# A hybrid attention encoder layer on one core: branch A's values as plain products kept on chip, branch B's rows stored in group order and merged by two heads and two tiles

## The chip, the core and the metric

The kernel runs on one core of a Trainium2 chip. The metric is the device time of one execution in microseconds (us). The engines are TensorE (PE in the profile: matrix products and transposes, with PEld its weight loads), VectorE (DVE), ScalarE (ACT), GpSimd (POOL) and SyncE (SP, which here only issues DMAs). Each engine works through its own queue in order and waits on semaphores; DMAs are issued from SP's and POOL's queues and move data between the chip's memory and DRAM.

## What is computed

The reference is one layer of an encoder on 1024 sample rows and 256 prompt rows of width 1024, in fp32:

```python
h = _rmsnorm(x, g_mix)
z = h @ w_in                                   # queries, keys, values of A and B, and 2 x 1024 gates
gates = jax.nn.sigmoid(z[..., o6:] + b_gate)
o_a, _ = _banded_attention(qa, ka, va, 128, 1, rel_bias[:, :8], sink)
o_b = _dilated_mixture(qb, kb, vb, rel_bias[:, 8:])
merged = gates[:, :, 0] * (o_a @ w_branch_a) + gates[:, :, 1] * (o_b @ w_branch_b)
x = x + merged @ w_out
h = _rmsnorm(x, g_mlp)
x = x + jnp.square(jax.nn.relu(h @ w_up)) @ w_down
return _rmsnorm(x, g_final)
```

Branch A has 8 heads of 64 in two groups that share keys and values, a window of 128 to both sides, and a sink. Branch B has three groups of four heads with dilations 1, 4 and 16; the group's sequence is taken apart by residues, each residue sees a band, and the three groups' outputs are mixed per head and row with a softmax of their log sums:

```python
alpha = jax.nn.softmax(jnp.stack(lses), axis=0)
o = jnp.sum(alpha[..., None] * jnp.stack(outs), axis=0)
```

## The kernel before

The 1280 rows are ten tiles of 128 (eight of the sample, two of the prompt) or three blocks of 512, 512 and 256 columns once transposed. fp32 accuracy comes from splitting: a value is rounded to fp32r by ScalarE (`split`, L184), the rest is taken by VectorE (L185), and a product is three fp32r products (low x high, high x low, high x high; `mm3`, L191). A matrix product on fp32 tiles without the split is called plain here.

The stages, by their place in the span: the norm and the value columns of w_in (0 to 120 us; `evac` writes the values to DRAM, A's split into two parts in scr_va, B's in scr_vb); 14 pairs of 128-column blocks of w_in (120 to 472; `PAIRS` at L46, `pair` at L805) which give queries, keys and 11 of the 16 gate blocks, each written to DRAM from a stage tile z; attention (472 to 876); branch B's product with w_branch_b and its gate (876 to 904); the out projection and norm (904 to 1060); the MLP (1060 to 1832). `entering` (L467) runs at the hooks of the last pair: it loads the first unit's queries and keys on SP, the normed input h, and prepares the first plain gate's weights (`prepare`: the load into raw, the ScalarE part L231, the VectorE part L235).

Attention is a list of 100 tiles: ten units of ten tiles, a unit being two heads. Units 0 to 3 are branch A, 4 and 5 are group 0 of branch B, 6 and 7 group 1, 8 and 9 group 2. For each tile `scores` (L890) multiplies queries and keys (L908 and L909 for A, L911 for B), adds the bias with the row maximum on VectorE (L915), negates the maximum (L920, L924) and takes the exponential on ScalarE (L926); one tile later `transposes` (L931) turns the probabilities on TensorE (L942) and evacuates them, and one more tile later `values_of` (L951) multiplies them with the values. A's values are [high | low] of 64 columns each as the stationary side and split probabilities as the moving one, 256 wide, two products per block of 128 keys (L962). The two halves of the output are added by ScalarE and VectorE (L968, L969), and the transposed result is stored by POOL into scr_a (L970). B's are plain products of 64 columns (L977), copied (L264 or L262, taken in turn) into o of 132 columns (two heads and the row's maximum and sum), which POOL stores into scr_b at strided rows (L986) or scr_b0 (L990). s has four buffers, o three.

Between the three steps of each tile a counter, `tick` (L1125), advances other work by hand-written rules. `logits` (L1005) are the products of the five gate blocks left over (11 to 15): 360 matmuls in 45 steps of eight, spread over tiles 0 to 39. From tile 42 on `sums_a` (L992) makes the reciprocal sums l_a and stores them transposed to scr_l; `fetch_gates` (L1040) loads the gates into mT; `fetch_a` (L1019) loads A's outputs and sums back on POOL's queue, multiplies them (L1036) and splits them into ohi and olo; `branch_a` (L1047) multiplies with w_branch_a and the gates (L1059). From tile 94 on `tail` (L1110) merges the three groups for one tile of 128 rows at a time: `merge` (L1063) loads r in two DMAs, takes minima, exponentials and weights on small tiles (L1071 to L1081), three products and two sums of 256 columns (L1085, L1092, L1093); `turn_merged` (L1099) transposes and splits. Most merges run after the last tile. The loop at L1183 multiplies with w_branch_b, columns outside and blocks inside, and applies the gates (L1194, L1196), with gate tiles sg loaded four steps ahead by SP (L1172).

Tiles live in pools with a fixed number of slots (tags m, w and q, of 4, 4 and 1 KB a partition). The order of instructions from the start of attention to the second half of the out projection is made by the scheduler from the program's order; ahead of that and behind it the program's order is kept.

Of the kernel before, what the change touches and what calls it, by code (L numbers as in the profile page):

```python
# [45 lines left out]
PAIRS = [(0, OFF_G), (P, OFF_G + P), (2 * P, OFF_G + 2 * P), (3 * P, OFF_G + 3 * P), (512, OFF_G + 4 * P)]  # L46
PAIRS += [(off + 256 * g, off + 256 * g + P) for g in (2, 1, 0) for off in (OFF_K, OFF_Q)]
PAIRS += [(OFF_G + P * c, OFF_G + P * c + P) for c in (5, 7, 9)]
# [48 lines left out]
def encoder_kernel(  # L97
# [155 lines left out]

    nm_a = const.tile([P, AH, NT], F32, name="nm_a")
# [14 lines left out]
    scr_a = dram.tile([AH * HD, T], F32, name="scr_a")  # L269
    scr_l = dram.tile([AH, T], F32, name="scr_l")  # L270
    scr_b = dram.tile([T, 2, 2, ROW], F32, name="scr_b")
# [118 lines left out]
    scr_va = dram.tile([T, 4 * HD], F32, name="scr_va")  # L390
    scr_vb = dram.tile([T, 3 * BH * HD], F32, name="scr_vb")
# [10 lines left out]
    def load_unit(u):  # L402
        st = {}
        if u < 4:
# [3 lines left out]
            if u % 2 == 0:  # L408
                kk = [slot("kk", (P, NS), F32R) for _ in range(2)]
                for i in range(2):  # L410
                    for r in HALVES:
                        nc.sync.dma_start(kk[i][r, :].bitcast(F32), scr_ka[g, i, :, :NS])
                        nc.sync.dma_start(shared["kp"][r, 2 * g + i, :].bitcast(F32), scr_ka[g, i, :, NS:])
                shared["k"] = [Pair(kk[i], shared["kp"][:, 2 * g + i, :]) for i in range(2)]
            if u:
                st["q"] = [Chunk("q", F32R) for _ in range(2)]
            else:
                rest = slot("qp", (P, 2, NP), F32R)
# [5 lines left out]
            if u == 0:  # L424
                shared["v"] = [slot("va", (P, 4 if t < 8 else 2, 2, 2, HD), F32R) for t in range(0, NT, 4)]
                for i, v in enumerate(shared["v"]):
                    src = scr_va[512 * i : min(T, 512 * i + 512), :].rearrange("(t p) c -> p t c", p=P)
                    nc.sync.dma_start(v.rearrange("p t g a d -> p t (g a d)").bitcast(F32), src)
# [8 lines left out]
        cols = slice(256 * g + P * i, 256 * g + P * i + P)  # L437
        sample, rest = scr_vb[:NS, cols], scr_vb[NS:, cols]
# [28 lines left out]
    def entering():  # L467

        nonlocal unit0
        yield  # L470
# [6 lines left out]
        yield  # L477
# [22 lines left out]
    with ExitStack() as pre:  # L500
# [99 lines left out]
        def evac(t, v, ps):  # L600
            rows = slice(P * t, P * t + P)
            vo = own("vo", (P, 512), n=2)
            if v == 0:
                nc.vector.tensor_copy(vo, ps)
                nc.gpsimd.dma_start(scr_vb[rows, :512], vo)
                return
            va = own("va", (P, 2, 2, HD), F32R, 2)
            split(va[:, :, 0, :], va[:, :, 1, :], ps[:, :P].rearrange("p (g d) -> p g d", g=2))
            nc.gpsimd.dma_start(scr_va[rows, :], va.rearrange("p g a d -> p (g a d)").bitcast(F32))
            nc.scalar.activation(vo[:, : 2 * P], ps[:, P : 3 * P], AF.Copy)  # L610
            nc.gpsimd.dma_start(scr_vb[rows, 512:], vo[:, : 2 * P])
# [100 lines left out]
    with ExitStack() as pre:  # L712
# [5 lines left out]
        class Rows:  # L718
# [5 lines left out]
            def begin(self):  # L724
                self.z = stage("z", (P, T), n=3)
# [19 lines left out]
        class Parts:  # L745
# [5 lines left out]
            def begin(self):  # L751
                self.z = [stage("z", (P, T), F32R, n=3) for _ in range(2)]
# [17 lines left out]
        class Gate:  # L770
# [5 lines left out]
            def begin(self):  # L776
                self.z = stage("z", (P, T), n=3)
# [80 lines left out]
    with ExitStack() as pre:  # L858
# [21 lines left out]
        def rows_out(g, n, gi):  # L880

            step = STEPS[g][gi >= NS]
            base, length = (0, NS) if gi < NS else (NS, NP)
            r, j = divmod(gi - base, length // step)
            first = base + r + step * j
            return slice(first, first + step * (n - 1) + 1, step)

        live, units = {}, {}

        def scores(u, t, tile):  # L890
# [4 lines left out]
            s = a3("s", bufs=4)  # L895
            m = small.tile([P, 2], F32, name="m", tag="m")
            o = a3("o", (P, ROW))
# [33 lines left out]
        def transposes(u, t, tile):  # L931
            W = tile[1]
            s, o = live[u, t]
            pt = a3("pt", (P, 6, P), bufs=2, dt=F32R if u < 4 else F32)
            low = wslot("pl", (P, 6, P), F32R) if u < 4 else None
# [13 lines left out]
            live[u, t] = (pt, low, o)  # L949

        def values_of(u, t, tile):  # L951
            st = units[u][0]
            pieces, W, _ = tile
            pt, low, o = live.pop((u, t))
            nb = W // P
            pv = bank("pv")
            if u < 4:
                for b in range(nb):
                    k = pieces[0][3] // P + b
                    v = st["v"][k // 4][:, k % 4, u // 2].rearrange("p a d -> p (a d)")  # L960
                    for p in (low, pt):
                        nc.tensor.matmul(  # L962
                            pv[:, : 2 * P], v, p[:, 2 * b : 2 * b + 2, :].rearrange("p h q -> p (h q)"),
                            start=b == 0 and p is low, stop=b == nb - 1 and p is pt,
                        )
                for h in range(2):
                    r, q = HALVES[h], slice(P * h, P * h + P)
                    nc.scalar.activation(o[r, :P], pv[HALVES[1], q], AF.Copy)  # L968
                    nc.vector.tensor_tensor(o[r, :P], pv[HALVES[0], q], o[r, :P], op=ALU.add)  # L969
                nc.gpsimd.dma_start(scr_a[P * u : P * u + P, P * t : P * t + P], o[:, :P])  # L970
                return
            g, i = divmod(u - 4, 2)
            for h in range(2):
                vc = HALVES[h]
                for p0, n, qa, ka in pieces:
                    for b in range(nb):
# [5 lines left out]
                        )  # L982
# [687 lines left out]
```

## Time and profile before

| | us |
|---|---|
| median of 3 runs | 1831.42 (1829.44 to 1832.73) |
| the profiled execution | 1833.65 |
| its span, first to last instruction | 1831.9 |
| TensorE busy | 1757.1 (96%), mean granted clock 0.970 |
| VectorE busy | 1000.4 (55%) |
| ScalarE busy | 754.9 (41%) |
| GpSimd busy | 528.1 (29%) |
| DMA | 255.46 MB in 187512 packets |

A share of busy time is a mean over stages that have different limits; the views by window show one stage at a time. Matmuls are pipelined, so the mean duration of one is longer than the time from one to the next, and a busy TensorE is not one at its peak. PEclk is the share of full speed that TensorE's clock was granted.

### The profile page before, as it was taken

The page shows a single profiled execution, that of the slowest core. Times are in us where ns is not written, and L with a number is a line of the kernel's source. Part 1 is how long each engine was busy: PE and PEld are TensorE (multiplying, and loading weights), DVE is VectorE, ACT ScalarE, POOL GpSimd, SP SyncE. Part 2 cuts the span into 40 slices and gives each one's busy share as a digit, 9 for nine tenths or more (in the row PEclk, how much of TensorE's full clock was granted, in tenths as well). Part 3 has the DMA queues.
Part 4 walks back from the last instruction along what each step waited for, and adds up shares of the span by engine and source line. Part 5 has one row for each costly group of instructions (what it writes and reads, how often), then busy time and mean ns, then how long its engine had stood idle before and what let it go on. Part 6 is the DMA issues. An engine that isn't in the chain of part 4 may idle for free.

```text
span 1831.9 us, 24545 instructions
## 1 busy us (share of the span) xinstructions
PE 1757.1 (96%) x9001; PEld 1464.9 (80%) x9001; DVE 1000.4 (55%) x1768; ACT 754.9 (41%) x1594; POOL 528.1 (29%) x438
## 2 busy tenths in 40 slices
PE   7999999999799989997899799999999999999998
PEld 6898888888688866765688688888888888888886
DVE  6633333322377743448846844554554796658575
ACT  6233332223376733543516533333333433233345
POOL 0221332212011231231010145555555551215050
PEclk9999999999899976998899999999999999999999
DMA  6416443332834574115611133444433864633433
GB/s 230 138 48 198 142 125 98 95 104 88 278 96 146 197 212 148 47 37 178 234 54 79 60 113 119 142 147 147 135 123 123 302 240 128 231 125 104 125 123 115
DMA packets 187512, 255.46 MB, mean 139 GB/s; under 512 B 15303, under 2 KB 116379, under 8 KB 187264
## 3 DMA queue, kind: packets, MB, share of 16 engines
q1 hardware_dynamic: 176576, 225.62, 37.7%
q0 software_dynamic: 9728, 26.18, 4.5%
q10 hardware_dynamic: 1088, 2.10, 0.3%
q8 instruction: 71, 1.16, 0.3%
q14 instruction: 49, 0.40, 0.1%
HBM read 167.66 MB, written 91.43 MB: 141 GB/s over the span
## 4 chain that ended last, share of the span: by engine, by line
PE 51%; DVE 4%; ACT 2%; DMA 2%; issue 1%; POOL 0%; SPq 0%; DVEq 0%; POOLq 0%; ACTq 0%
PE dn L345 19%; PE x L345 9%; PE mm L191 7%; PE pv L345 5%; PE z L345 4%; PE y L345 2%; PE sc L911 2%; PE pv L977 2%; PE pt L942 1%; DMA scr_b<-o 1%; DMA raw<-in_w_down_dram 0%; DVE ulo L185 0%; DMA raw<-in_w_out_dram 0%; DVE clo L312 0%; DVE sg L1194 0%
## 5 line engine op out<-in xcount | busy, mean ns | idle before, releaser
L345 PE MATMUL dn<-dhi,ulo 128*128 128x512 f32 x448 | 174.6, 390 | 2.7 <-DVE ulo L185 2.7
L376 POOL TENSOR_TENSOR tb<-raw 128x512 f32<-128x512 f32 x30 | 39.0, 1301 | 473.0 <-DMA raw<-in_w_in_dram 170.1
L312 DVE TENSOR_TENSOR wlo<-ta,whi 128x1024 fp32r<-128x1024 f32 x30 | 56.6, 1887 | 215.7 <-ACT whi L310 215.7
L345 PE MATMUL dn<-dlo,uhi 128*128 128x512 f32 x448 | 174.3, 389 | 0.0
L345 PE MATMUL dn<-dhi,uhi 128*128 128x512 f32 x448 | 174.3, 389 | 0.0
L345 PE MATMUL x<-chi,wlo 128*128 128x512 f32 x424 | 167.3, 395 | 6.9 <-ACT phi L184 6.9
L345 PE MATMUL x<-clo,whi 128*128 128x512 f32 x424 | 167.0, 394 | 0.0
L345 PE MATMUL x<-chi,whi 128*128 128x512 f32 x424 | 166.3, 392 | 0.0
L312 DVE TENSOR_TENSOR wlo<-raw,whi 128x1024 fp32r<-128x1024 f32 x60 | 93.2, 1553 | 111.1 <-ACT whi L310 111.1
L345 PE MATMUL pv<-phi,wlo 128*128 128x256 f32 x480 | 135.6, 283 | 0.9 <-ACT u L1558 0.9
L345 PE MATMUL pv<-phi,whi 128*128 128x256 f32 x480 | 135.8, 283 | 0.0
L345 PE MATMUL pv<-plo,whi 128*128 128x256 f32 x480 | 135.8, 283 | 0.0
L915 DVE CUSTOM_DVE_ANT_0 s<-sc,bias 128x256 f32<-128x256 f32 (+2 forms) x200 | 77.5, 404 | 64.4 <-PE pt L942 29.4
L185 DVE TENSOR_TENSOR ulo<-uraw,uhi 128x1024 fp32r<-128x1024 f32 x56 | 95.1, 1718 | 11.7 <-ACT uhi L184 11.7
L345 PEld LDWEIGHTS dn<-dhi,ulo 128*128 128x128 f32 x448 | 84.1, 188 | 21.3 <-DVE ulo L185 3.8
L345 PEld LDWEIGHTS x<-chi,wlo 128*128 128x128 f32 x424 | 80.7, 190 | 22.9 <-ACT phi L184 7.3
L345 PEld LDWEIGHTS dn<-dlo,uhi 128*128 128x128 f32 x448 | 84.1, 188 | 17.4
L345 PEld LDWEIGHTS dn<-dhi,uhi 128*128 128x128 f32 x448 | 84.1, 188 | 17.3
L345 PEld LDWEIGHTS pv<-phi,wlo 128*128 128x128 f32 x480 | 91.9, 191 | 3.4 <-ACT u L1558 1.1
L345 PEld LDWEIGHTS x<-chi,whi 128*128 128x128 f32 x424 | 80.5, 190 | 17.2
L345 PEld LDWEIGHTS pv<-plo,whi 128*128 128x128 f32 x480 | 91.9, 191 | 2.3
L345 PEld LDWEIGHTS x<-clo,whi 128*128 128x128 f32 x424 | 80.7, 190 | 15.1
(329 smaller groups left out, 4607.0 us busy)
## 6 DMA issues: line engine op xcount, KB each, us to landing
scr_u<-u SPq DMA_DIRECT2D x112, 320.0 KB, 2.6
uraw<-scr_u SPq DMA_DIRECT2D x56, 512.0 KB, 4.6
raw<-in_w_in_dram SPq DMA_DIRECT2D x33, 512.0 KB, 5.1
raw<-in_w_up_dram SPq DMA_DIRECT2D x32, 512.0 KB, 5.2
raw<-in_w_down_dram SPq DMA_DIRECT2D x28, 512.0 KB, 6.2
uraw<-scr_u SPq DMA_DIRECT2D x28, 256.0 KB, 4.4
scr_g<-z SPq DMA_DIRECT2D x11, 640.0 KB, 7.6
scr_qa<-z SPq DMA_DIRECT2D x16, 320.0 KB, 6.5
```

The costliest lines, as they stand in the source:

```text
L185: nc.vector.tensor_tensor(lo, src, hi.bitcast(F32), op=ALU.subtract)
L191: nc.tensor.matmul(ps, a, b, start=i == 0, stop=i == len(seq) - 1)
L312: nc.vector.tensor_tensor(lo, src, hi.bitcast(F32), op=ALU.subtract)
L345: nc.tensor.matmul(ps, a, b, start=first and i == 0, stop=last and i == len(seq) - 1, skip_group_check=True)
L376: nc.gpsimd.tensor_tensor(tb[:, 0], b12, b11, op=ALU.subtract)
L911: nc.tensor.matmul(ps[p0 : p0 + n, :W], st["q"][rows, qa : qa + n], st["k"][rows, ka : ka + W], start=True, stop=True,)
L915: nc.vector.tensor_tensor_reduce(s[:, h, :W], ps[:, :W], bias[:, h, c0 : c0 + W], 1.0, -3.0e38, op0=ALU.add, op1=ALU.max, accum_out=m[:, h ...
L942: nc.tensor.transpose(ps[:, P * (i % 4) : P * (i % 4) + P], s[:, h, P * b : P * b + P], ident)
L977: nc.tensor.matmul(pv[p0 : p0 + n, HD * h : HD * h + HD], pt[:, 2 * b + h, p0 : p0 + n], v_at(st, ka // P + b)[:, vc], start=b == 0, stop= ...
```

## The change

- The order of the pairs in `PAIRS`: queries of A pair with each other, and gates 1 to 10 pair at the end. The stage tile z has four buffers in place of three.
- The values of A and B go to one DRAM tensor (scr_v) with one copy and one store per tile, A's no longer split.
- `entering` issues the load of the first plain gate's weights at the first hook, ahead of the loads of unit 0, and prepares one hook earlier. Six steps of `logits` (48 matmuls) are taken ahead of the first scores. The other 39 are spread over tiles 0 to 59 in place of 45 over tiles 0 to 39.
- A's values are plain products of 64 columns, 208 where there were 208 of 256 columns; the probabilities are copied and not split. The result goes into rows on chip (`oa`, five m slots for two tiles each) and not to scr_a. `turn_a` scales the rows by l_a on VectorE, transposes them (four per tile) and splits them from PSUM into ohi and olo. scr_a, scr_l and `fetch_a` are gone.
- `window` runs `turn_a` and `branch_a` densely from tile 62 on, every step to tile 73 and two of five after that; `branch_a` goes by block and half of the columns.
- The order of units is 0, 1, 2, 3, 8, 6, 4, 9, 7, 5, so that the first heads of the three groups are done after tile 69 and the second heads at the end.
- B's rows are stored in the order in which the group's tiles produce them; `merge(i, t)` merges one pair of heads for two tiles of 128 rows, with r of [rows, two tiles, three groups]: 76 loads of r where there were 20, two products of 384 columns and two sums of 256 in place of three and two of 256, ten merges as before. The turned columns are put back in order by a strided split, 20 of 128 columns in place of ten of 256. The first pair of heads is merged in tiles 74 to 97, the second from tile 95 on.
- o is made only for branch B, s has three buffers. The branch-B loop has blocks outside and columns inside, and both halves of w_branch_b are fetched ahead.

The core of the diff:

```diff
     def entering():
         nonlocal unit0
+        fetch()
         yield
         unit0 = load_unit(0), *load_bias(0, wslot)
...
-        yield
         prepare()
         yield
...
             for i, e, ps in banks:
-                dst, src = pt[:, i:e, :], ps[:, : P * (e - i)].rearrange("p (i q) -> p i q", q=P)
-                if u < 4:
-                    split(dst, low[:, i:e, :], src)
-                else:
-                    copy(dst, src)
+                copy(pt[:, i:e, :], ps[:, : P * (e - i)].rearrange("p (i q) -> p i q", q=P))
...
             for h in range(2):
-                vc = HALVES[h]
+                vc = HALVES[h if u >= 4 else u // 2]
                 for p0, n, qa, ka in pieces:
                     for b in range(nb):
                         nc.tensor.matmul(
...
+            if u < 4:
+                copy(oa(t)[:, P * u : P * u + P], pv[:, :P])
+                return
             copy(o[:, : 2 * HD], pv[:, : 2 * HD])
             for p0, n, qa, ka in pieces:
                 if g:
-                    nc.gpsimd.dma_start(scr_b[rows_out(g, n, qa), g - 1, i, :], o[p0 : p0 + n, :])
+                    nc.gpsimd.dma_start(scr_b[g - 1][qa : qa + n, i, :], o[p0 : p0 + n, :])
...
+        def turn_a(t):
+            if t in (0, 4, 8):
+                o_hi.block(t // 4)
+                o_lo.block(t // 4)
+            o = oa(t)
+            o3 = o.rearrange("p (h d) -> p h d", h=AH)
+            nc.vector.tensor_tensor(o3, o3, l_a[:, :, t].unsqueeze(2).to_broadcast([P, AH, HD]), op=ALU.mult)
+            yield
+            ps = bank("pt")
+            for k in range(4):
+                nc.tensor.transpose(ps[:, P * k : P * k + P], o[:, P * k : P * k + P], ident)
+            p3 = ps.rearrange("p (k q) -> p k q", k=4)
+            per = o_hi.per(P * t)
+            for k in range(0, 4, per):
+                split(o_hi.at(k, P * t, P, per), o_lo.at(k, P * t, P, per), p3[:, k : k + per, :])
+            yield
...
+        def window():
+            for t in range(4):
+                yield from turn_a(t)
+            w_as[0] = weight()
+            w_as[1] = weight(0)
+            for b in range(3):
+                turns = then(*[turn_a(t) for t in range(4 * b + 4, min(4 * b + 8, NT))])
+                for _ in branch_a(b, range(4)):
+                    yield
+                    steps_of(turns, 2)
+                    yield
+            w_as[2] = weight(0)
+            w_as[3] = weight(0)
+            for b in range(3):
+                yield from branch_a(b, range(4, KC))
...
+        def merge(i, t):
+            r = wslot("r", (P, 2, 3, ROW))
+            for j in range(2):
+                if t < 8:
+                    a = P // 8 * (t + j)
+                    src = scr_b0[t + j][:, i, :].rearrange("(q m) c -> m q c", m=8), (
+                        scr_b[0][:NS, i, :].rearrange("(r q m) c -> m r q c", r=4, m=2)[:, :, a : a + 16]), (
+                        scr_b[1][:NS, i, :].rearrange("(r q) c -> r q c", r=8)[:, a : a + 16])
+                    for m in range(2):
+                        nc.sync.dma_start(r[64 * m : 64 * m + 64, j, 1, :], src[1][m])
+                    nc.sync.dma_start(r[:, j, 2, :], src[2])
+                    nc.sync.dma_start(r[:, j, 0, :], src[0])
+                    continue
...
+            for j in range(2):
+                o = r[:, j, :, : 2 * HD].rearrange("p g (h d) -> p g h d", h=2)
+                nc.vector.tensor_tensor(o, o, e[:, j].unsqueeze(3).to_broadcast([P, 3, 2, HD]), op=ALU.mult)
+            m = a3("mg", (P, 2, P), bufs=2)
+            nc.vector.tensor_tensor(m, r[:, :, 0, : 2 * HD], r[:, :, 1, : 2 * HD], op=ALU.add)
+            nc.vector.tensor_tensor(m, m, r[:, :, 2, : 2 * HD], op=ALU.add)
...
-        order = [(u, t, tile) for u in (0, 1, 2, 3, 8, 9, 6, 7, 4, 5) for t, tile in enumerate(tiles_of(u))]
+        order = [(u, t, tile) for u in (0, 1, 2, 3, 8, 6, 4, 9, 7, 5) for t, tile in enumerate(tiles_of(u))]
...
         def tick(i):
             n = ticks[0]
             ticks[0] += 1
-            if i < 40:
-                if (n + 1) * 45 // 120 > n * 45 // 120:
+            if i < 60:
+                if (n + 1) * 39 // 180 > n * 39 // 180:
                     next(fill, None)
-            elif i > 44:
-                if n % 3 == 0 and n < 168 or n % 9 == 0 and ticks[0] < 300:
-                    next(side)
-                if i > 94 or i == 94 and n % 3 == 2:
-                    next(last, None)
+                return
+            if i > 61 and (i < 74 or n % 5 < 2):
+                next(side, None)
+            if 74 <= i < 98:
+                if n % 3 == 1:
+                    next(merges[0], None)
+            if done[0] < 20 and i > (94, 96, 98, 99, 101)[done[0] // 4]:
+                next(merges[1])
+                done[0] += 1
...
+        steps_of(fill, 6)
```

More of the change, by code (lines that the diff above doesn't have):

```diff
@@ L953, in values_of @@
             pieces, W, _ = tile
-            pt, low, o = live.pop((u, t))
+            pt, o = live.pop((u, t))
             nb = W // P
             pv = bank("pv")
[L957 to L971, printed above, removed]
             g, i = divmod(u - 4, 2)
             for h in range(2):
-                vc = HALVES[h]
+                vc = HALVES[h if u >= 4 else u // 2]
                 for p0, n, qa, ka in pieces:
```

220 lines of the change are left out of this document (85 added, 135 removed).

## The prediction

> **What bounds the kernel now.** I read the page's slices first (TensorE is busy nearly everywhere, but its clock dips around attention), then the busy time by stage from the view of windows, then the timeline and the chain of waits at the two places where TensorE stands still.
>
> ```profile
> core 0: us, PE busy (x) PEld busy (x) DVE busy (x) ACT busy (x) POOL busy (x), PEclk, DMA share, GB/s
> 120.00:472.00 352.00, 352.00 (x1856) 300.50 (x1855) 110.91 (x115) 110.47 (x160) 85.60 (x73) 1.00 0.40 124
> 472.00:490.00 18.00, 6.34 (x23) 5.02 (x22) 2.17 (x6) 3.28 (x4) 1.47 (x2) 0.62 0.89 311
> 490.00:640.00 150.00, 147.56 (x933) 127.37 (x931) 107.23 (x366) 109.66 (x321) 24.38 (x44) 1.00 0.47 153
> 640.00:700.00 60.00, 51.98 (x213) 37.18 (x211) 30.93 (x115) 25.71 (x88) 20.62 (x34) 0.75 0.65 192
> 700.00:760.00 60.00, 58.03 (x321) 39.52 (x320) 22.69 (x113) 24.16 (x85) 13.82 (x25) 0.80 0.35 105
> 760.00:847.00 87.00, 86.21 (x558) 62.85 (x558) 44.65 (x218) 42.92 (x144) 28.53 (x54) 1.00 0.26 71
> 847.00:880.00 33.00, 18.08 (x76) 13.26 (x75) 25.41 (x92) 6.33 (x15) 0.05 (x1) 0.66 0.62 210
> 880.00:904.00 24.00, 24.00 (x124) 20.53 (x123) 21.87 (x40) 13.02 (x24) 0.00 (x0) 0.97 0.88 290
> ```
>
> The stages outside 472 to 904 us are full of products that the change leaves alone: in 120 to 472 TensorE is busy for 352.00 of 352.00 us at clock 1.00. The change there only reorders column pairs and stores the values in another form, so I cost it at nothing; the cover is TensorE itself, and without it the values' store, the only part with less work, would gain, not cost. All of the sum comes from the attention stage and its two ends. There TensorE is held up in three places: at the start (6.34 us busy of 18), in the first part of branch B (clock 0.75 and 0.80), and in the merges (18.08 of 33).
>
> **The start of attention.** These rows are from the timeline; columns are start, duration, engine, line, and in brackets the idle time before.
>
> ```profile
> 482.02 1.06 ACT L231 ACTIVATE whi<-raw 128x1024 fp32r<-128x1024 f32 x1 [13.88 <-DMA raw<-in_w_in_dram]
> 484.38 0.79 PE L191 MATMUL mm<-hhi,wlo 128*128 128x512 f32 x1 [11.66 <-DVE wlo L235]
> 487.66 0.42 DVE L915 CUSTOM_DVE_ANT_0 s<-sc,bias 128x256 f32<-128x256 f32 x1 [3.33 <-DMA scr_g<-z]
> ```
>
> The weights of the first plain gate arrive late, ScalarE waits for them with the last pair's sigmoid queued behind, and the store of that gate (scr_g) holds the first eviction until 487.66. The change issues this load at the first hook, ahead of SP's loads of unit 0, so both steps come earlier. 48 of the 360 gate products are put ahead of the first scores; at 24 x 0.227 + 24 x 0.113 (prices below) they take 8.2 us, and they cover the loads of unit 0. From 472.7 I expect about 10 us to the first eviction, so 483: **-5 us**. If unit 0's loads are still the last to land it is 0; if they were early, -7, since the 8.2 us remain in the way.
>
> **Branch A's tiles (490 to 640).** First the prices. The first two rows are windows of TensorE alone, the next ones the timeline of a branch-B tile, then one row of the chain of waits in branch B, the rest groups in 490 to 640.
>
> ```profile
> 1600.00:1800.00 200.00, 199.26 (x880) 1.00 0.36 115
> 150.00:450.00 300.00, 300.00 (x1586) 1.00 0.39 121
> 815.09 0.49 PE L942 MATMUL pt<-ident,s 128*128 128x128 f32 x3
> 815.51 0.45 PE L977 MATMUL pv<-v,pt 128*64 128x64 f32 x8
> 815.89 0.50 PE L191 MATMUL mm<-ohi,wlo 128*128 128x512 f32 x1
> 817.18 1.10 PE L977 MATMUL pv<-v,pt 128*128 128x64 f32 x8
> 818.22 0.49 PE L911 MATMUL sc<-k,q 64*128 64x256 f32 x2
> 729.69 1.90 PE pv L977 x8
> L962 PE MATMUL pv<-pl,va 128*128 128x256 f32 x103 | 28.7, 305 | 1.7 <-DVE o L969 0.9
> L962 PE MATMUL pv<-pt,va 128*128 128x256 f32 x102 | 25.9, 281 | 0.0
> L191 PE MATMUL mm<-hhi,whi 128*128 128x512 f32 x76 | 30.9, 406 | 0.0
> L191 PE MATMUL mm<-plo,whi 128*128 128x256 f32 x40 | 11.8, 294 | 0.0
> L185 DVE TENSOR_TENSOR pl<-pt 128x512 fp32r<-128x512 f32 x40 | 27.6, 689 | 15.4 <-ACT pt L184 14.7
> L969 DVE TENSOR_TENSOR o<-pv,o 64x128 f32<-64x128 f32 x78 | 21.9, 281 | 10.6 <-ACT o L968 9.5
> ```
>
> The mean durations of matmuls overlap, so I price by rate. All matmuls of 1600 to 1800 are 512 wide: 200 / 880 = 0.227 us. In 150 to 450 they are two 512-wide to one 256-wide, 300 / 1586 = 0.189, which leaves 0.113 for a 256-wide one. A plain fp32 product is not one record: lines 973 to 980 issue four for a tile of two blocks, the trace shows x8, and from 817.18 to the next start at 818.22 they take 1.04 us, so 0.26 us for each 128x64 product. That is more than twice the 0.113 of the 256-wide fp32r product that it replaces. The change replaces 208 by 208: 208 x (0.26 - 0.113) = **+30 us** of TensorE work in this stage. The ends: 0.095 each (815.51 to 815.89, the half-width stationary tile) gives -4 us, and 0.47 (1.90 us for eight records, at a low clock) gives +75. I take the row with the same tile and width, at full clock.
>
> On this price the Trainium skill differs. "FP8 and Floating Point Precision", TensorE Precision Notes, says that true FP32 takes 4 passes through the array. Four passes of 64 columns are one pass of 256, so by that page the exchange is free, an estimate of 0 us in place of +30; it is the first rival below. The row of 1.04 us for four products speaks against it.
>
> Against this, gate products leave the stage. In before all 346 that the groups show (226 512-wide, 120 256-wide) run here, 226 x 0.227 + 120 x 0.113 = 65 us. In after 26 of the 39 steps of eight fall here: 208 x 0.189 = 39 us. So -26 + 30 = +4 us of TensorE work. VectorE loses the split of the probabilities and the second half of the output (64 and 78 instructions; the rows show 27.6 and 21.9 us) and gets half the copies back, so from 107 to about 70 us in the stage; ScalarE goes from 110 to about 78. Priced by width (scores at 0.113 and 0.170, 210 transposes at 0.11 to 0.14, 0.49 us for three being the high end), TensorE's work here was 136 to 143 of 150 us, so 7 to 14 us went to waits. With both helpers a third lighter I give back 9 of them: +4 - 9 = **-5 us**. What is late next is TensorE itself.
>
> **Branch B's tiles (640 to 847).** The rows are one of the chain, one of the waits in 640 to 720, two groups of 760 to 847, two of 640 to 847, and one of 847 to 910.
>
> ```profile
> 718.19 5.69 DMA scr_b<-o
> ACT ohi L184 <- DVE oa L1036: 12.8, 4, 4.0
> L191 PE MATMUL mm<-ohi,wlo 128*128 128x512 f32 x29 | 12.5, 432 | 0.0
> L924 DVE TENSOR_SCALAR o<-m 128x2 f32<-128x2 f32 x26 | 4.3, 164 | 5.4 <-DMA scr_b<-o 5.4
> L915 DVE CUSTOM_DVE_ANT_0 s<-sc,bias 128x256 f32<-128x256 f32 x48 | 19.7, 422 | 20.5 <-PE pt L942 7.6 <-PE sc L911 7.2 <-issue 3.9
> L264 DVE COPY o<-pv 128x128 f32<-128x128 f32 x58 | 16.8, 290 | 36.3 <-PE pv L977 36.2
> L1085 DVE TENSOR_TENSOR r<-r,e 128x256 f32<-128x256 f32 x18 | 6.6, 419 | 0.1
> ```
>
> In 760 to 847, at clock 1.00, TensorE is full: 26 tiles (the count of L924) and about 87 wide and 48 narrow branch-A products, 25 us. So a tile costs (87 - 25) / 26 = 2.4 us there, with two blocks in most. The tiles of one block have half the records, so about 1.2. Sixty tiles are then some 107 us. After adds all of branch A (8 blocks x 12 x (2 x 0.227 + 0.113) = 54 us), 13 gate steps (104 x 0.189 = 20 us), and 40 transposes of branch A's rows (4 to 6 us): 186 us of work. Before had 58 tiles (L264) and 49 us of branch A, about 155 in its 207 us; most of the other 52 were lost ahead of 760 to two things that the change takes away: branch A's outputs come back through scr_a and scr_l (the waits of ohi for oa, 12.8 us in 640 to 720) on the same POOL queue as the stores whose landing frees o (5.69 us at 718). After turns branch A's rows on chip: ten VectorE scalings of 128x512 and ten splits from PSUM, near 0.69 us each by L185, beside TensorE's 96 us of work in tiles 60 to 80. The last twenty tiles have no filler: TensorE 42 us, VectorE about 1.25 us a tile (L915, the copy, two small ones) plus some seven of the ten merges at 3.8 us (two products near 0.55, two sums 0.42, two splits 0.29, eight small ones 0.16), so 25 + 27 = 52 us, and VectorE is the bound. Sum: 186 + 10 + 6 lost = 202, **-5 us**. The 76 loads of the merges (20 before) go to SP, whose queue in this stretch holds only the loads of the last two units, and each costs some 0.4 us of issue; if they land late nothing hides it, which is the second rival.
>
> **The tail.** The last tile's L924 from the view of that line, a wait and a group of 847 to 910, and pieces of the chain (start, duration).
>
> ```profile
> L924 DVE TENSOR_SCALAR o<-m x1: 161/161/161, 840.5 to 840.5; 128x2 f32<-128x2 f32 x1
> ACT obhi L184 <- PE pt L1106: 14.1, 7, 5.1
> 851.56 2.86 DMA r<-scr_b
> 875.98 11.72 PE mm L191 x48
> L1194 DVE TENSOR_TENSOR sg<-mm,sg 128x512 f32<-128x512 f32 x16 | 11.1, 691 | 2.9 <-PE mm L191 2.1 <-ACT sg L1177 0.4
> 899.19 7.31 DMA raw<-in_w_out_dram
> 908.90 1.22 PE mm L191 x2
> ```
>
> From the last tile's L924 at 840.5 to the out projection at 908.9 are 68 us. After leaves three of the twenty half merges behind the last tile: two run while its rows are stored and loaded (about 8 us: exponentials, transposes, products, a store and a load of 2 to 3 us each), the third takes 3.8, so 13 us. Then the 24 gate steps of branch B follow, bound by VectorE (two instructions of 0.69 or 0.42 us each, 29 us), and the load of w_out with its split, which still ends last: 7 to 9 us. 13 + 29 + 9 = 51: **-17 us**. If the loads of the gates wait behind the merges' loads, -8; if w_out is early, -23.
>
> **Sum.** -5 - 5 - 5 - 17 = -32 us against the profiled execution's 1833.65 (span 1831.9), so 1801.7; the median of the runs lies 2.2 lower, so **1800**. The bounds of its own terms give 1785 to 1815.
>
> **The rivals.**
> 1. Plain products cost no more than the ones they replace. For it: the low row at 0.095. Then A's tiles have 25 us less to do, and VectorE at 70 us is far off: 1775. 12 in 100.
> 2. The last twenty tiles wait for the merges: 7680 rows of 528 bytes, and the o buffers that wait for stores (5.4 us already in 760 to 847). At 3.5 us a tile in place of 2.6 that is +18: 1820. 20 in 100. For it speaks that these tiles have nothing else for TensorE.
> 3. Slower: the clock. Branch B has 186 us of TensorE work, so a mean clock c adds 186/c - 186 us. It eats the 32 us at c = 0.85. Before had 0.75 and 0.80 over 120 us. At 0.80 it is +46: 1848. For it: short matmuls and waits, as there; against it: the waits of 640 to 720 go, and 490 to 640 with as many short matmuls kept 1.00. 17 in 100. The Trainium skill has a rule for this side ("TensorE: Matmul & The Clock Gate", Part 4: PE-mode transpose): transposes do not count as busy for the clock gate. By that rule the added transposes and the last tiles lower the clock; the stage of 490 to 640, with 210 transposes among 933 matmuls, shows no such thing.
> 4. Nothing to see: the +30 us in A is not paid back by lighter helpers and the tail gives only its -8; 1831. 9 in 100.
>
> **How the numbers follow.** The forecast has 42 in 100, the rivals 12, 20, 17 and 9. The range of 1772 to 1836 holds the forecast and rivals 1, 2 and 4, 83 in 100, and leaves out the slow one. A measurement of this kernel tells about 0.2% (3.7 us) from no change. Faster: 42 + 12 + 20 = 74; within: 9; slower: 17.
>
> **What would show it.** First eviction near 483 at clock 1.00; eight records of A's 128x64 products in about 1.0 us; 145 us for A's tiles with TensorE full and VectorE near 70 us; clock above 0.95 up to tile 80; VectorE busier than TensorE in the last twenty tiles; the out projection about 51 us after the last L924. The forecast is wrong if the products take 0.5 us for eight records, or if the clock of branch B is below 0.85.

## The result and the profile after

The changed kernel is 1.2% slower: 1855.7 us (median of 4 runs, 1851.08 to 1861.67) against 1832.08 (4 runs), a ratio of 1.0124 with a 95% interval of 1.0083 to 1.0166. The profiled execution took 1851.08, its span is 1849.3. The forecast was 1800.

The first view is the windows of the changed kernel, cut near the starts of tiles 0, 40, 60 and 80, near the last tile's start, and near the out projection. A tile's start is that of L908 or L912 (L920 or L924 of before), the instruction right behind the eviction of its scores. Columns as in the prediction.

```profile
core 0: us, PE busy (x) PEld busy (x) DVE busy (x) ACT busy (x) POOL busy (x), PEclk, DMA share, GB/s
482.00:614.00 132.00, 132.00 (x971) 123.81 (x970) 70.80 (x263) 76.28 (x222) 5.06 (x7) 1.00 0.36 113
614.00:685.00 71.00, 63.34 (x397) 47.63 (x395) 30.92 (x144) 26.80 (x104) 14.72 (x26) 0.90 0.58 184
685.00:787.00 102.00, 97.71 (x588) 78.70 (x590) 49.42 (x188) 37.61 (x125) 17.61 (x32) 0.98 0.29 88
787.00:876.00 89.00, 75.88 (x309) 51.31 (x309) 37.79 (x189) 32.27 (x110) 15.99 (x30) 0.52 0.25 74
876.00:926.00 50.00, 32.64 (x168) 26.39 (x168) 37.69 (x94) 22.76 (x55) 3.15 (x6) 0.80 0.66 215
```

The same cuts in the kernel before:

```profile
488.00:636.00 148.00, 145.56 (x913) 126.05 (x911) 104.58 (x355) 108.39 (x312) 25.22 (x44) 1.00 0.48 154
636.00:716.00 80.00, 71.98 (x304) 51.79 (x302) 39.69 (x155) 32.28 (x113) 24.88 (x41) 0.72 0.61 180
716.00:779.00 63.00, 60.91 (x393) 41.96 (x392) 25.31 (x130) 28.82 (x102) 16.65 (x30) 0.92 0.26 75
779.00:840.00 61.00, 60.32 (x378) 43.46 (x378) 30.59 (x155) 31.53 (x102) 18.96 (x36) 1.00 0.24 64
840.00:904.00 64.00, 49.08 (x240) 39.12 (x239) 53.22 (x155) 22.07 (x47) 3.16 (x6) 0.81 0.72 238
```

The start and branch A's tiles got shorter: the first eviction starts at 482.5 (487.7), and tiles 0 to 39 take 131 us (148) with TensorE full at clock 1.00. So did the tail (51.5 us against 63.1). All of that and more is lost in branch B's tiles: 261 us against 204, where tiles 60 to 79 take 102 us and the last twenty 88. In these last twenty TensorE's clock was 0.52.

What the tiles wait for shows in the view of L912, the instruction that first writes a tile's o, in the changed kernel, and of L924 in the one before:

```profile
L912 DVE TENSOR_SCALAR o<-m x60: 157/165/178, 614.4 to 875.2; 128x2 f32<-128x2 f32 x60
...
its engine sat idle before it (us, times) until:
  DMA scr_b__82<-o: 9.0, 5
  DMA scr_b<-o: 9.0, 6
  DMA scr_b__83<-o: 6.7, 5
who waited for it (us, times):
  ACT s L914: 54.3, 36
```

```profile
L924 DVE TENSOR_SCALAR o<-m x60: 157/164/290, 636.3 to 840.5; 128x2 f32<-128x2 f32 x60
...
its engine sat idle before it (us, times) until:
  DMA scr_b<-o: 11.9, 10
```

VectorE stood idle for 24.7 us until a store of o had landed, and ScalarE waited 54.3 us for L912. The timeline shows the loop (VectorE rows, then POOL's queue, both of the changed kernel):

```profile
614.36 0.16 DVE L912 TENSOR_SCALAR o<-m 128x2 f32<-128x2 f32 x1
...
617.39 0.16 DVE L912 TENSOR_SCALAR o<-m 128x2 f32<-128x2 f32 x1
...
619.29 0.16 DVE L912 TENSOR_SCALAR o<-m 128x2 f32<-128x2 f32 x1
...
623.62 0.16 DVE L912 TENSOR_SCALAR o<-m 128x2 f32<-128x2 f32 x1
...
625.03 0.17 DVE L912 TENSOR_SCALAR o<-m 128x2 f32<-128x2 f32 x1 [0.65 <-DMA scr_b__83<-o]
```

```profile
620.83 0.58 POOL L957 DMA_DIRECT2D scr_b__83<-o  x1 [7.30 <-ACT o L263]
622.02 0.56 POOL L957 DMA_DIRECT2D scr_b__83<-o  x1 [0.61 <-ACT o L263]
```

The first three tiles take the three buffers at 614.36, 617.39 and 619.29. The first store is issued at 620.83 and lands at 622.73; the fourth L912 runs at 623.62, behind two scalings of branch A's rows on VectorE. The store issued at 622.02 lands at 624.90, and the fifth L912, which the trace names as waiting for it, runs at 625.03. From there on a tile can start only when the one three ahead is stored, so on average it takes at least a third of the time for which a tile holds its o, from its L912 to the landing of its store. By these starts and landings a tile of 40 to 59, 60 to 79 and 80 to 99 holds its o for 9.6, 14.8 and 12.4 us on average. A third of that is 3.2, 4.9 and 4.1 us, and the tiles step by 3.5, 5.1 and 4.6.

### The profile page after: what moved, and what is told of

Its sections match the earlier page's. It is cut to its first block, busy times and chain, and to the rows that moved or that the text cites. A ratio compares the mean times of both kernels' runs of the same rounds, so it can differ in the third digit from the quotient of the medians.

```text
span 1849.3 us, 24708 instructions
## 1 busy us (share of the span) xinstructions
PE 1773.8 (96%) x9248; PEld 1493.8 (81%) x9248; DVE 968.0 (52%) x1683; ACT 722.8 (39%) x1515; POOL 489.8 (26%) x372
## 4 chain that ended last, share of the span: by engine, by line
PE 47%; DVE 3%; ACT 2%; DMA 1%; issue 1%; POOL 0%; DVEq 0%; ACTq 0%; SPq 0%
PE dn L345 19%; PE x L345 9%; PE mm L191 6%; PE pv L345 5%; PE z L345 4%; PE y L345 2%; DVE v L1531 0%; DVE clo L312 0%; DMA r<-scr_b 0%; PE pv L945 0%; ACT xn L1313 0%; DMA scr_b<-o 0%; ACT chi L310 0%; DVE ulo L185 0%; DMA v<-scr_x 0%
## 5 line engine op out<-in xcount | busy, mean ns | idle before, releaser
L345 PEld LDWEIGHTS x<-clo,whi 128*128 128x128 f32 x424 | 80.2, 189 | 14.8
```

Source lines behind the costliest of these rows:

```text
L345: nc.tensor.matmul(ps, a, b, start=first and i == 0, stop=last and i == len(seq) - 1, skip_group_check=True)
```

## The experiments

Theory C: the last twenty tiles have no filler, so the clock falls to half and TensorE's own work sets the pace. Theory W: waits hold the tiles, and the clock only follows. The first four runs were to tell these apart; then theory W was narrowed to theory L, the loop of three o buffers. Times of tiles are those of the profiled execution, from tile start to tile start; the last column runs from the last L912 (L924) to the first product with the low part of w_out.

| run | median us | ratio to before, 95% interval | tiles 0-39 | 40-59 | 60-79 | 80-99 | to out projection |
|---|---|---|---|---|---|---|---|
| before | 1832.08 | | 147.8 | 80.6 | 63.2 | 60.5 | 63.1 |
| changed | 1855.7 | 1.0124 (1.0083 to 1.0166) | 131.1 | 70.7 | 102.1 | 88.1 | 51.5 |
| spread | 1843.7 | 1.0048 (1.0031 to 1.0065) | 131.2 | 72.2 | 78.7 | 87.6 | 58.4 |
| dummy | 1849.25 | 1.0077 (1.0057 to 1.0097) | 131.2 | 71.8 | 108.5 | 76.5 | 57.1 |
| a_alone | 1828.29 | 0.9962 (0.9946 to 0.9979) | 151.2 | 62.9 | 73.2 | 72.0 | 55.6 |
| late | 1870.42 (one) | | 131.2 | 76.3 | 106.9 | 78.8 | 66.1 |
| q6 | 1857.65 (one) | | 131.5 | 69.7 | 107.3 | 90.4 | 51.2 |
| o4 | 1817.5 | 0.9919 (0.9901 to 0.9937) | 130.2 | 57.4 | 95.8 | 66.8 | 57.4 |
| more_o | 1803.94 | 0.9829 (0.9796 to 0.9863) | 131.2 | 51.3 | 95.5 | 56.4 | 57.2 |
| spread_o6 | 1789.28 | 0.9757 (0.9735 to 0.9778) | 130.5 | 51.5 | 59.7 | 77.3 | 60.8 |
| spread_o6_m1 | 1789.39 | 0.9767 (0.9749 to 0.9785) | 131.0 | 51.3 | 59.7 | 75.2 | 60.1 |
| a_alone_o6 | 1800.85 | 0.9825 (0.9811 to 0.984) | 151.2 | 56.8 | 57.1 | 67.7 | 56.8 |
| before_o6 | 1791.38 | 0.9773 (0.9755 to 0.9792) | 148.6 | 57.9 | 51.9 | 54.9 | 61.3 |
| early | 1789.09 | 0.9746 (0.9712 to 0.978) | 143.3 | 64.7 | 56.1 | 54.9 | 61.9 |

**spread**

```diff
-            if i > 61 and (i < 74 or n % 5 < 2):
+            if i > 61 and n % 5 < 2:
```

> Branch A's products go on at two of five steps to tile 99 and are not done by tile 82. Theory C (the clock): in the changed kernel tiles 80 to 99 took 88 us because TensorE, without a filler, fell to half clock from 788 to 874 us and its own work set the pace. Then here the clock stays above 0.9 in these tiles, they take 65 to 75 us with more work in them, tiles 60 to 79 some 75 us (102 before), and the kernel runs in 1805 to 1825. Theory W (waits): these tiles are held by the buffers of o, the merges' loads and VectorE, and the clock only follows. Then they still take 85 us or more, what is won is the filler that moves out of tiles 60 to 79, and the kernel runs in 1825 to 1840.

The last two windows of tiles:

```profile
685.00:764.00 79.00, 71.78 (x392) 54.74 (x392) 39.55 (x175) 36.41 (x124) 18.15 (x34) 0.86 0.37 109
764.00:852.00 88.00, 79.83 (x500) 62.35 (x498) 45.97 (x202) 33.17 (x111) 15.77 (x30) 0.93 0.38 119
```

The last twenty tiles had their filler and a clock of 0.93, and still took 88 us. What was won is what left tiles 60 to 79. That is W's outcome for the tiles, and C's 65 to 75 did not come; the time of 1843.7 lies above the range of either. The filler is itself work in these tiles: with six buffers the same order (spread_o6, below) takes 77.3 us there, so this run alone puts only some 10 of the 88 us down to waits.

**dummy**

```diff
+            if i > 80 and i < 100:
+                ps = bank("mm", "warm")
+                for _ in range(2):
+                    nc.tensor.matmul(ps, w_as[3][0][:, 0, :P], w_as[3][1].rearrange("p a b -> p (a b)")[:, :512], start=True, stop=True)
```

> Only extra work: in tiles 81 to 99 two 512-wide products a step that nobody reads, 114 products, 26 us of TensorE at full clock. Theory C: they hold the clock up, tiles 80 to 99 take 70 to 78 us in place of 88 in spite of the added work, and the kernel gains 10 us or more over the changed one. Theory W: nothing is gained, tiles 80 to 99 take 88 us or more.

```profile
793.00:870.00 77.00, 70.04 (x419) 47.97 (x419) 39.17 (x191) 32.23 (x109) 16.00 (x30) 0.93 0.32 100
```

With 26 us of useless work and a clock of 0.93 the tiles took 77 us and not 88. So the clock has a part in it, as C said. But the kernel gained some 6 us by the medians and not 10 (the intervals of the two ratios overlap), tiles 60 to 79 took 6 us longer, and 77 us is still far from the 56 of the next run.

**more_o**

```diff
-N_M, N_Q, N_W = 33, 8, 10
+N_M, N_Q, N_W = 33, 6, 10
-            o = a3("o", (P, ROW), bufs=3) if u >= 4 else None
+            o = a3("o", (P, ROW), bufs=6) if u >= 4 else None
```

> Six buffers for o in place of three, paid for by two of the eight small slots. Theory W: the waits of L912 for stores (25 us in tiles 40 to 99) go, tiles 40 to 59 fall from 71 to 55 us or less and tiles 80 to 99 by 10 us or more. Theory C: tiles 80 to 99 stay within 4 us of 88 at clock 0.5; tiles 40 to 59 may gain a few us.

The view of L912 and the windows of its branch-B tiles:

```profile
L912 DVE TENSOR_SCALAR o<-m x60: 157/164/284, 614.0 to 817.2; 128x2 f32<-128x2 f32 x60
...
its engine sat idle before it (us, times) until:
who waited for it (us, times):
  ACT s L914: 20.1, 21
```

```profile
614.00:665.00 51.00, 50.89 (x384) 40.51 (x382) 29.95 (x135) 26.41 (x104) 14.15 (x25) 1.00 0.76 251
665.00:761.00 96.00, 95.28 (x599) 77.34 (x598) 50.65 (x194) 37.79 (x126) 18.18 (x33) 1.00 0.34 99
761.00:817.00 56.00, 47.02 (x296) 32.71 (x294) 35.79 (x186) 30.41 (x111) 15.76 (x30) 0.83 0.30 91
```

The waits for stores are gone, and with them 52 us by the medians (the four runs lie between 1799 and 1811). With three buffers 24 of 57 reuses of a buffer came within 0.5 us of the landing that freed it; with six none comes sooner than 1.8 us. Of the 58 us that the tiles gave back, 19 lie in tiles 40 to 59, 32 in the last twenty, and only 7 in tiles 60 to 79: these still take 95.5 us, because TensorE is busy for 95.28 of 96 us with the dense branch-A products. Tiles 40 to 59 are at clock 1.00, not 0.90, and the last twenty at 0.83, not 0.52: the clock followed the waits. Nothing was done to the clock or to the filler. The change also takes one of the four buffers of s; more_o keeps three, and TensorE is full in its tiles 40 to 79, so s doesn't hold these.

**a_alone** takes the changed kernel and puts back branch B's strided stores, the merges of one tile, the order of units and the loop over w_branch_b of before.

```diff
-        order = [(u, t, tile) for u in (0, 1, 2, 3, 8, 6, 4, 9, 7, 5) for t, tile in enumerate(tiles_of(u))]
+        order = [(u, t, tile) for u in (0, 1, 2, 3, 8, 9, 6, 7, 4, 5) for t, tile in enumerate(tiles_of(u))]
...
+            if i < 40:
+                if (n + 1) * 39 // 120 > n * 39 // 120:
+                    next(fill, None)
+            elif i > 44:
+                if n % 3 == 0:
+                    next(side, None)
+                if i > 94 or i == 94 and n % 3 == 2:
+                    next(last, None)
```

> Branch A's part and the gates' start as in the changed kernel; branch B's stores, merges, order of units and the loop over w_branch_b as before the change; branch A's products at one of three steps from tile 45 on. The changed kernel does A's forty tiles in 132 us where the kernel before took 148, and starts 5 us earlier. Theory C: with filler up to tile 90 the clock stays up and the tail is that of before, so 1805 to 1820. Theory W says nothing else here than that the o buffers still wait: 1815 to 1832.

1828.29: A's part with three buffers is worth 4 to 10 us, in W's range and outside C's. Here all 39 steps of gate products stay in tiles 0 to 39, and these take 151.2 us: the difference to the 131.1 of the changed kernel is 20 us, the 13 steps x 8 x 0.189 that were moved.

**before_o6** has the two edits of more_o in the kernel before.

```diff
-            o = a3("o", (P, ROW))
+            o = a3("o", (P, ROW), bufs=6)
```

> The kernel before with six buffers for o in place of three, paid for by two of the eight small slots. Theory L (the loop of o): a branch-B tile holds its o from L924 to the landing of its store, and with three buffers a tile cannot take less than a third of that time. In the kernel before that is 8.3 to 9.5 us, and tiles 60 to 99 step by 3.0 to 3.3 us, so it is bound by it too: with six, tiles 40 to 99 take 185 to 198 us in place of 204 and the kernel runs in 1812 to 1825. Rival: only the changed kernel is bound by it, because it has no filler or a denser one; then 1828 to 1836 here.

```profile
637.00:695.00 58.00, 54.64 (x259) 39.87 (x258) 35.64 (x143) 29.31 (x106) 23.66 (x39) 0.82 0.72 194
695.00:747.00 52.00, 51.71 (x401) 38.73 (x399) 27.86 (x130) 30.93 (x109) 16.88 (x31) 1.00 0.48 149
747.00:802.00 55.00, 54.91 (x402) 43.83 (x402) 32.75 (x165) 30.63 (x102) 19.79 (x38) 1.00 0.27 69
```

Some 42 us, more than theory L had said: tiles 40 to 99 took 165 us in place of 204. So the kernel before was held by the same loop all along, in its first branch-B tiles too, where the prediction had blamed the detour of A's outputs: ScalarE still waits 12.9 us for these (12.8 before), and tiles 40 to 59 fall from 80.6 to 57.9 us all the same. Both kernels gain by six buffers, some 52 and 42 us, and the comparison turns round: 1803.94 with the change, 1791.38 without.

**spread_o6** is more_o with the edit of spread.

```diff
-            if i > 61 and (i < 74 or n % 5 < 2):
+            if i > 61 and n % 5 < 2:
```

> Six buffers for o and branch A's products at two of five steps up to tile 99. Theory L: with six buffers the tiles follow TensorE's work, which is the same as in more_o; only the clock (0.5 in 798 to 825 and 832 to 852 there) can still be won. Tiles 40 to 99 take 195 to 203 us, tiles 80 to 99 hold a clock above 0.9, 1792 to 1804 in all. If the density of the filler mattered by itself, as theory C had it, 10 us or more below more_o.

1789.28, below the expected range. Tiles 40 to 99 took 188.5 us in place of 203.3, the clock was 1.00, 1.00 and 0.98 in their three parts. Against more_o it is 15 us by the medians: once the buffers are there, the dense window costs what TensorE lost at the end by waiting and at clock 0.83. Against before_o6 the intervals overlap.

**o4**

```diff
-N_M, N_Q, N_W = 33, 8, 10
+N_M, N_Q, N_W = 33, 7, 10
-            o = a3("o", (P, ROW), bufs=3) if u >= 4 else None
+            o = a3("o", (P, ROW), bufs=4) if u >= 4 else None
```

> Four buffers for o in the changed kernel, paid for by one of the eight small slots. Theory L: the step is a quarter of the holding time where that is above the work: tiles 40 to 59 in 53 to 60 us (71 with three, 51 with six), tiles 80 to 99 in 62 to 75 (88 and 56), 1815 to 1833 in all. If six buffers only won by another order of instructions or by the slots given up, no such step between three and six.

As expected: 70.7, 57.4 and 51.3 us in tiles 40 to 59 with three, four and six buffers, 88.1, 66.8 and 56.4 in the last twenty. 70.7 x 3/4 is 53.0, so four buffers bring most of what the loop says.

**late**

```diff
-            if 74 <= i < 98:
-                if n % 3 == 1:
-                    next(merges[0], None)
-            if done[0] < 20 and i > (94, 96, 98, 99, 101)[done[0] // 4]:
-                next(merges[1])
-                done[0] += 1
```

> The changed kernel with all ten merges behind the last tile, three buffers for o. Theory L: tiles 80 to 99 still take 70 us or more, at clock 0.5 for the most part, since the store of each tile's o closes the loop and no merge is in it; the tail grows by seven to eight merges of some 4 us, so 1860 to 1885. If the merges' loads and their VectorE work held the tiles, tiles 80 to 99 fall to 55 us or less.

The last twenty tiles still took 78.8 us without a merge among them, so the merges don't hold them; they cost 9 of the 88 us. The tail grew by 15 us.

**a_alone_o6** is a_alone with the two edits of more_o.

```diff
-            o = a3("o", (P, ROW), bufs=3) if u >= 4 else None
+            o = a3("o", (P, ROW), bufs=6) if u >= 4 else None
```

> a_alone (branch A's part and the gates' start as changed, branch B's stores, merges and order of units as before) with six buffers for o. Theory L: its tiles 40 to 99 took 208 us with three buffers, where the work was that of the kernel before and 4 us of transposes; with six they take 166 to 175 us (165 in before_o6), tiles 0 to 39 stay at 151, and the kernel runs in 1783 to 1797, level with before_o6 at 1791 within its start and the price of the plain products. If the change of branch B is what loses against before_o6, this run is level with it; if that of branch A does, it is 8 us or more above.

1800.85, 9.5 us above before_o6: the second outcome. A's tiles take 151 us with 312 gate products among them (39 steps of eight), where before_o6 has some 350 of its 360 there and takes 148.6, and tiles 40 to 99 182 us, not 166 to 175. So A's part alone costs against before_o6 when the loop is open, though it started 6 us earlier. How much of the 17 us in tiles 40 to 99 is due to where its filler came to lie wasn't separated.

**spread_o6_m1** drops the second heads' merges from spread_o6's tiles.

```diff
-            if done[0] < 20 and i > (94, 96, 98, 99, 101)[done[0] // 4]:
-                next(merges[1])
-                done[0] += 1
```

> spread_o6 with the second heads' five merges all behind the last tile. Theory L with an addition M: in tiles 94 to 99 the merges' first VectorE instruction waits for the loads of r (5.0 and 2.4 us in spread_o6) and the next tile's L903 stands behind it in VectorE's queue. Then tiles 80 to 99 fall from 77 to 62 to 68 us and the tail grows by three merges, 8 to 12 us: 1780 to 1792 in all. If the merges cost only their own work, tiles 80 to 99 fall by 8 us or less and the kernel is not faster than 1789.

The addition M falls: tiles 80 to 99 lost 2 us, and the time is the same. The wait that had suggested it is real, as this timeline of VectorE in spread_o6 shows (the trace names a load of x as what ended it, not one of r), but it did not set the pace:

```profile
787.65 0.16 DVE L1074 TENSOR_TENSOR mm__7594<-r 128x4 f32<-128x4 f32 x1 [5.03 <-DMA x<-in_x_sample_dram]
787.74 0.42 DVE L903 CUSTOM_DVE_ANT_0 s<-sc,bias 128x256 f32<-128x256 f32 x1
```

**q6**, the control:

```diff
-N_M, N_Q, N_W = 33, 8, 10
+N_M, N_Q, N_W = 33, 6, 10
```

> Control: the changed kernel with two of the eight small slots given up and three buffers for o as it has. Theory L: nothing is won, 1848 to 1862, tiles 40 to 99 in 250 to 270 us. If the slots or the order of instructions made more_o fast, this run comes near 1804.

1857.65 and 267 us for tiles 40 to 99. It is the buffers of o, not the slots.

**early** adds to before_o6 the change's start alone.

```diff
         nonlocal unit0
+        fetch()
         yield
...
-        yield
         prepare()
...
-                if (n + 1) * 45 // 120 > n * 45 // 120:
+                if (n + 1) * 39 // 120 > n * 39 // 120:
...
+        steps_of(fill, 6)
```

> before_o6 (the kernel before with six buffers for o) with the one part of the change that no other run has alone: the first plain gate's weights are loaded at the first hook, and 48 gate products run ahead of the first scores. By the traces the start gains 5 us, and of the 346 gate products in tiles 0 to 39 some 38 leave, 7 us: tiles 0 to 39 from 148.6 to 140 to 143, the first eviction near 483, 1776 to 1784 in all. If these tiles are not held by TensorE, only the start is gained: 1785 to 1788.

The start came (the first eviction at 482.8) and so did tiles 0 to 39 (143.3 against 148.6), 10 us together; tiles 40 to 79 gave them back (120.8 us against 109.8). In both kernels ScalarE waits 12.9 us there for A's outputs that come back from DRAM (ohi for oa); what made the rest of these tiles longer was not followed up. 1789.09 lies above both expected ranges and is not distinguishable from before_o6 at 1791.38. Its tiles 0 to 39 also give a price that was missing: they have nearly the start and all 312 gate products of a_alone_o6 and take 143.3 us where that takes 151.2, so branch A's part as changed costs some 8 us there, and that kernel is 12 us slower in all.

## Why the prediction was wrong

**The step that failed** is in branch B's tiles: "most of the other 52 were lost ahead of 760 to two things that the change takes away". It summed TensorE's and VectorE's work and took the wait for o (5.69 us at 718) for something that POOL's loads of A's outputs had caused; the waits in 760 to 847 (5.4 us) it put into rival 2 alone. Six buffers in the kernel before, with these loads still there, took 40 us out of the same tiles. The three buffers held branch B in both kernels, and the change left their number as it was. The sum has no term for them.

The sums of TensorE's work hold where the loop is open. more_o took 51.3, 95.5 and 56.4 us for the three twenties; the prediction's 186 us were 96 for tiles 60 to 79, 42 for the last twenty and so 48 for the first. That the last twenty come near its 52 us is luck: it had VectorE as the bound, and VectorE is busy for 35.79 of 56 us there, TensorE for 47.02 at clock 0.83. Its 1800 is near the time of more_o, 1803.94, and not that of the change; that too is partly luck, since A's tiles gained more than forecast and the tail less. Its own sign of being wrong came: the clock of branch B, 614 to 876, was 0.80, below the 0.85 that it names.

Point by point:
- **The start**: -5 us forecast, -5.2 measured (482.5 against 487.7), and 18.00 of 18.00 us busy in 472 to 490 as this row of the changed kernel has it.

```profile
472.00:490.00 18.00, 18.00 (x102) 15.63 (x101) 4.44 (x16) 6.10 (x14) 1.46 (x2) 1.00 0.98 347
```

- **Branch A's tiles**: -5 forecast, -16.7 measured. The mechanism was right, the price of the plain product too high. Two rows of the changed kernel's timeline:

```profile
541.03 1.45 PE L945 MATMUL pv<-va,pt 128*128 128x64 f32 x12
542.29 0.36 PE L896 MATMUL sc<-kp,qp 128*128 128x256 f32 x1
```

  Twelve records, six products, take 1.26 us to the next start: 0.21 each, not 0.26. That is +20 us in place of +30. VectorE is at 70.8 us and ScalarE at 76.3, forecast 70 and 78; and TensorE is the bound, 132.00 of 132.00 us. The gain is less than the work that left these tiles: six gate steps went ahead of the first scores and 13 into branch B's tiles, 29 us at 8 x 0.189 us a step. The estimate from the Trainium skill's "FP8 and Floating Point Precision", TensorE Precision Notes, four passes of 64 columns for one of 256 and so no cost at all, was rival 1: the row gives 0.21 against 0.113, so the measurement decides against it.
- **Branch B's tiles**: -5 forecast, +56.5 measured (260.8 against 204.3). With the dense filler between a tile's steps, tiles 60 to 79 took 102 us where before had 63 and less filler; then the last twenty took 88 without any. With six buffers in both kernels 38.5 of the 56.5 us remain (203.2 against 164.7): 19.7 for the gate products and about 4 for the transposes that came here, and 15 for the dense window, by spread_o6. The other 18 are the loop, which costs 57.6 us here and 39.6 in the kernel before.
- **The tail**: -17 forecast, -11.6 measured to the first product with w_out's low part. The prediction's 908.90 is a product of w_out's second piece; to the same product it is 54.3 us (929.45) in place of 68.3, so -14. The last load took 6.28 us where 2 to 3 were assumed, the last store 2.57: these pieces are from the changed kernel's chain.

```profile
881.91 2.57 DMA scr_b<-o
884.53 6.28 DMA r<-scr_b
...
896.77 2.83 DMA sg<-scr_g
```

  Of the gain nothing is left against before_o6: 60.8 us in spread_o6, 61.3 there.
- The rest of the span, from the first product with w_out on, was 5.7 us shorter (922.8 against 928.5), which was not forecast. About 4 of the 5.7 lie in the first half of the out projection: before, TensorE waits 1.30 and 0.76 us there for the split of w_out's second piece and its clock is 0.85 in 903.5 to 915; after, it doesn't wait, at clock 1.00 in 926.5 to 938. -5.2 - 16.7 + 56.5 - 11.6 - 5.7 = +17.3, the difference of the two spans (17.4).
- **Rival 3, the clock**, had the sign and nearly the time (1848), and the clock did fall to 0.52 in the last twenty tiles. But as a first cause it was wrong: more_o let the clock come back without touching it. The clock does have a part: dummy, which raised it to 0.93, took 12 us off the 88 with 26 us of added work in the same tiles. That it works through the loop (at half speed a tile's steps are longer, so it holds its o longer) is argued, not shown. The Trainium skill's rule that goes with this rival (transposes don't count as busy in the same way, "TensorE: Matmul & The Clock Gate", Part 4: PE-mode transpose) was not put to a test by itself: more_o has the same transposes and clock 1.00 in 614 to 761.
- **Rival 2**, late merges, had one part right, the o buffers that wait for stores, and one wrong: without the merges (late) the last twenty tiles took 79 us.

With the loop open, the change as a whole is worth nothing that these runs can tell: spread_o6 1789.28, before_o6 1791.38. By stages it moves time: -6 at the start, -18 in A's tiles, +24 in B's, and the last is about as much as the 13 gate steps (19.7 us) that came there and the 40 transposes (4 us) that were added. early, spread_o6, spread_o6_m1 and before_o6, alike within their intervals, are the fastest versions found, 2.3 to 2.5% below the kernel before, and nearly all of that is the buffers.

## What to carry to other kernels

Where tiles pass through a small number of buffers that are freed by a store, work out the bound of that loop first: the time from a buffer's first write to the landing of its store, divided by the number of buffers. If it is near the step that the trace shows, sums of engine work don't give the time until a buffer is added, and filler put between a tile's steps can make the loop longer (9.6 us of holding in tiles 40 to 59, 14.8 in 60 to 79). Where one engine is full for the whole step, as in tiles 60 to 79 of more_o, another buffer brings little. A falling TensorE clock next to such waits is to be treated as an effect until an experiment that removes the waits leaves it low.

## What was not expected of the hardware

- A plain fp32 product of a 128x128 stationary tile with 64 columns took 0.21 us in a row of six, against 0.113 for a 256-wide fp32r one, and is two records in the trace.
- The clock was 0.50 from 788 to 874 us in the changed kernel, though TensorE counts as busy for 73.89 of these 86 us; spread's last twenty tiles had 79.83 of 88 us and a clock of 0.93. A high count of busy time did not mean a high clock here.
- A load of 64 rows of 528 bytes took SP about 0.54 us to issue, two in 1.08, in the changed kernel's timeline:

```profile
834.10 1.08 SPq L1062 DMA_DIRECT2D r<-scr_b__82  x2
...
835.22 0.58 SPq L1063 DMA_DIRECT2D r<-scr_b__83  x1
```

  The prediction had taken 0.4 us. SP was not the bound: from 787 to 880 its queue stood 68.8 us waiting for stores.
